# Convolutions as keys, values, queries, and the delta rule's prologue written among their products

## The chip, the cores and the metric

The kernel runs on one core of a Trainium2 chip. TensorE (PE) multiplies matrices, VectorE (DVE) and ScalarE (ACT) do elementwise work, GpSimd (POOL) a little more of it, and SyncE (SP) starts the transfers from memory. The metric is the device time of one execution in microseconds (us); lower is better.

## The reference

Two stacks of two layers each run one after the other on one sequence of 512 positions and 1024 channels. The change lies in the mixer of the second stack's layers. There the input `h` is multiplied by one wide matrix and the columns are split among three mixers: a sliding-window attention, a gated linear scan (HGRN) and a gated delta rule. The delta rule is, shortened:

```python
cqkv = jax.nn.silu(causal_depthwise_conv(cqkv, conv_w))          # width 4, 768 channels
cq, ck, cv = jnp.split(cqkv, [256, 512], axis=-1)                # 4 heads of 64 each
cq = l2norm(cq) * 64 ** -0.5
ck = l2norm(ck)
beta = jax.nn.sigmoid(cb)
g = -jnp.exp(a_log) * jax.nn.softplus(ca + dt_bias)
o_c = gated_delta_chunked(cq, ck, cv, beta, g)
# per chunk: v_new = u - w @ state ; o = q_dec @ state + qk @ v_new
#            state = g_last * state + k_dec.T @ v_new
# u, w: solutions of one triangular system whose matrix is made of the keys, beta and g
out_c = rmsnorm_2(o_c, gdn_norm) * jax.nn.silu(cg)
mixed = jnp.concatenate([out_a, out_b, out_c], axis=-1)
return mixed @ w_out
```

The matrix of the triangular system needs the keys and the gates only. The values enter as a right-hand side, the queries in `qk` and in the output.

## The kernel before

All activations are kept transposed, as tiles of 128 channels by 512 positions. Weights come as tiles of 128 by 1024 numbers: a transfer into one of three raw buffers (`wraw`), a cast by ScalarE to the upper half (`whi`, line 381) and a subtraction by VectorE for the lower half (`wlo`, line 382), each half in one of four buffers. A product (`mm3`, lines 406 to 408) is three matmuls for each of 8 tiles of input, 24 for one tile of 128 output channels. `lin_f` does such products tile by tile and hands each result, in one of four banks of PSUM with the tag `mm`, to a function `ev`.

The program is one straight list of instructions. A planner at build time puts them into the queues of the engines: the place in the list is the priority, and an instruction that the planner thinks ready may go ahead of an earlier one that it thinks is not, if a buffer of its tag is free. On the chip each queue then runs as it was written. `weave` takes turns between Python generators at each `yield`, so it sets the order in the list.

`second_mixer` computes, in this order: the inputs of the HGRN scan and the scan itself (`hgrn`), with the products for the windowed attention and the gates listed around it; the attention's rotation and factors up to its yield of "ready" (`swa`); `last[0]()`, which transposes and splits the scan's result into `y_b`; the six products `w[4:10]` for queries (outputs 4, 5), keys (6, 7) and values (8, 9), each followed by its convolution (`conv`: a copy by ScalarE, one scaling and three multiply-adds by VectorE, a tanh, one more multiply-add); then `gdn`, woven with the rest of `swa`. The output projection follows.

`gdn` begins with the gates (lines 1351 to 1373). Sums of squares of queries and keys go to one bank (line 1379), GpSimd raises them to the power -0.5 (`power`, line 1384), and `spread2` (a copy at line 682, four transposes at 676) turns a factor into a full tile with which the key tiles are multiplied (line 1390). The key tiles are copied into zero-padded tiles `kz`. For the right-hand sides `rhs` values and keys are transposed (`to_f`, line 713) and multiplied by columns (1412, 1415, 1417). Then four blocks of 128 positions are worked, woven step by step. The first steps of `block` are: decay matrix from transposed gates (1438, 1441) and a transfer of identities into one `whi` and one `wlo` buffer; key products (1450) and their scaling (1452); a transpose (1457) and two masked copies (1458, 1459); query-key products (1463, 1464) and their transpose (1468). Then six rounds of two matmul steps and a transpose (1476, 1481, 1487, with copies at 1477, 1482, 1488), the solution with the right-hand sides (1492), and `wt` (1501). The state then runs over the blocks, and the output is made.

Of the kernel before, what the change touches and what calls it, by code (L numbers as in the profile page):

```python
# [13 lines left out]
ALU = mybir.AluOpType  # L14
# [3 lines left out]
P = 128  # L18
SEQ = 512
NB = SEQ // P  # L20
# [3 lines left out]
EPS = 1e-6  # L24
# [225 lines left out]
class Net:  # L250
# [1092 lines left out]
        last.append(lambda: [self.split(early.to_f([hs[:, b].rearrange("p a b -> p (a b)") for b in range(NB)])) for hs in done])  # L1343


    def gdn(self, x, cg, ba, l, out):
        nc, V, G = self.nc, self.nc.vector, self.nc.gpsimd
        T = nc.tensor
        early = self.using(pst="mm")

        sh = (P, NB, 4)
        beta, u, g = (self.small(sh, n, 2) for n in ("gb", "gu", "gg"))
# [10 lines left out]
        ps = self.ps("mm")  # L1363
# [3 lines left out]
        gc, eg, el, gl = (self.small(sh, n, 2) for n in ("gc", "geg", "gel", "ggl"))  # L1367
        f = lambda y: y.rearrange("p a b -> p (a b)")
# [2 lines left out]
        V.tensor_tensor(f(el), ps[:, 16:32], f(gc), op=ALU.subtract)  # L1371
        nc.scalar.activation(out=eg, in_=gc, func=AF.Exp)
        nc.scalar.activation(out=el, in_=el, func=AF.Exp)

        st = self.ps("mm")
        for i in range(4):
            sq = self.square(x[i], "ns")
            for b in range(NB):
                T.matmul(st[:, 8 * b + 2 * i:8 * b + 2 * i + 2], sq[:, b * P:(b + 1) * P], self.bd64[:, 0:65:64], start=True, stop=True)
        rs_ = self.small((P, 32), "gms", 2)  # L1380
        V.tensor_scalar(rs_, st[:, 0:32], EPS, None, op0=ALU.add)
        rs3, rn = rs_.rearrange("p (a b) -> p a b", a=NB), self.small((P, NB, 8), "grn", 2)
        def power(c):
            G.tensor_tensor(rn[:, :, c], rs3[:, :, c], self.nhalf[:, 0:32].rearrange("p (a b) -> p a b", a=NB)[:, :, c], op=ALU.pow)

        power(slice(4, 6))
        power(slice(6, 8))
        for i in range(2, 4):
            ps = early.spread2(rn[:, :, 2 * i:2 * i + 2])
            V.tensor_tensor(x[i], x[i], ps, op=ALU.mult)  # L1390
            yield
        power(slice(0, 4))
        rq = self.small((P, NB, 4), "grq", 2)
        V.tensor_scalar(rq, rn[:, :, 0:4], 0.125, None, op0=ALU.mult)
        q, k, vf = x[0:2], x[2:4], x[4:6]
        kz2 = [self.big((P, 2, SEQ), "gk") for _ in range(2)]
        kz = [kz2[h // 2][:, h % 2, :] for h in range(4)]
        for h, t in enumerate(kz):
            r, n = slice(64 * (h % 2), 64 * (h % 2) + 64), slice(64 - 64 * (h % 2), 128 - 64 * (h % 2))
            G.memset(t[n, :], 0.0)  # L1400
            nc.scalar.copy(t[r, :], k[h // 2][r, :])

        eb = self.small(sh, "geb", 2)
        V.tensor_tensor(eb, beta, eg, op=ALU.mult)
        rhs, kd = [], []
        for i in range(2):
            hh = slice(2 * i, 2 * i + 2)
            bc = lambda y: y[:, :, hh].unsqueeze(3).to_broadcast([P, NB, 2, 64])
            r = self.big((P, NB, 2, 128), name="grhs")
            ps = early.to_f([vf[i][:, b * P:(b + 1) * P] for b in range(NB)])  # L1410
            v4 = ps.rearrange("p (a b c) -> p a b c", a=NB, b=2)
            V.tensor_tensor(r[:, :, :, 0:64], v4, bc(beta), op=ALU.mult)
            ps = early.to_f([k[i][:, b * P:(b + 1) * P] for b in range(NB)])
            k4 = ps.rearrange("p (a b c) -> p a b c", a=NB, b=2)
            V.tensor_tensor(r[:, :, :, 64:128], k4, bc(eb), op=ALU.mult)
            t = self.t((P, NB, 2, 64), name="gkd")
            V.tensor_tensor(t, k4, bc(el), op=ALU.mult)
            rhs.append(r)
            kd.append(t)
            yield  # L1420
        m0, m1, m2 = self.mats("lv64", 4), self.mats("lv4", 4), self.mats("later", 2)
# [6 lines left out]
        p4 = lambda y: y.rearrange("p (a b) -> p a b", a=4)  # L1428
        QT, uw = [None] * NB, [None] * NB
        wt = [self.t(name="gwt") for _ in range(2)]  # L1430

        yield

        def block(b):
            s = slice(b * P, (b + 1) * P)
# [67 lines left out]
                    nc.scalar.copy(wt[i][:, s], ps[:, i * P:(i + 1) * P])  # L1503
            yield

        yield from weave(*(block(b) for b in range(NB)))

        sbd = {}
        for i in range(2):
            state = None  # L1510
            for c in range(NB - 1):
                ps = self.ps("mx")
                for p in range(2):
                    r = slice(64 * p, 64 * p + 64)
# [6 lines left out]
                else:  # L1521
                    m = self.t((P, P), name="gmt", tag="x")
                    G.memset(m, 0.0)
                    for p in range(2):
                        r = slice(64 * p, 64 * p + 64)
                        V.scalar_tensor_tensor(m[r, r], self.ident[r, r], gl[r, c, 2 * i + p:2 * i + p + 1], ps[r, 64 + 64 * p:128 + 64 * p],
                                               op0=ALU.mult, op1=ALU.subtract)
# [10 lines left out]
                for p in range(2):  # L1538
                    r = slice(64 * p, 64 * p + 64)
# [3 lines left out]
        for b in range(NB):  # L1543
# [16 lines left out]
            else:  # L1560
                t = self.t((P, 4, 64), name="got", tag="x")
                V.tensor_tensor(t, o3(po[:, 256:512]), eg[:, b, :].unsqueeze(2).to_broadcast([P, 4, 64]), op=ALU.mult)
                V.tensor_tensor(hs[:, 0], t, o3(p2[:, 0:256]), op=ALU.add)
            r = self.head_rstd(hs, (1, 4), rq[:, b:b + 1, :])
# [142 lines left out]
    def second_mixer(self, x, l):  # L1707
        nc, V, G = self.nc, self.nc.vector, self.nc.gpsimd
        keep = {}

        def ev(o, ps):
            if 4 <= o < 10:
                keep[o] = L.conv(ps, self.vec("conv_w2", l)[:, 4 * (o - 4):4 * (o - 4) + 4], 3, None)
                return
            t = keep[o] = L.t(name="u")
            if o < 4:
                nc.scalar.copy(t, ps)
                return
# [12 lines left out]

        def gate(t, ps):

            nc.scalar.activation(out=t, in_=ps, func=AF.Tanh, scale=0.5)
            V.scalar_tensor_tensor(t, t, 1.0, ps, op0=ALU.add, op1=ALU.mult)

        def evt0(b, ps):
            nc.scalar.copy(bv[:, b, :], ps[:, 0:256])
            gate(bg[:, b, :], ps[:, 256:512])

        def evt1(b, ps):
            nc.scalar.copy(av[:, b, :], ps[:, 0:128])
            gate(cg[:, b, :], ps[:, 128:384])
            V.tensor_copy(ba[:, b, :], ps[:, 384:392])

        w = self.tiled("win2_f", l, KD)
        y_a, y_c, last = [], [], []

        def gains(t, n):
            t4 = t.rearrange("p a (b c) -> p (a b) c", b=4)  # L1750
            G.tensor_tensor(t4, t4, self.row(n, l).unsqueeze(1).to_broadcast([P, 16, 64]), op=ALU.mult)

        self.lin_f(w[0:4], x, ev, wide=4)
        gh = self.using("m", "mx").hgrn([keep[2], keep[3]], [keep[0], keep[1]], bv, bg, l, last)
        for n, _ in enumerate(self.lin_t_steps(self.d["win2_t0"][l], x, 512, evt0)):
            if n + 1 in (7, 8):
                next(gh)
        for n, _ in enumerate(gh):
            if n == 2:
                gains(bg, "hgrn_norm")  # L1760
        self.lin_t(self.d["win2_t1"][l], x, 392, evt1)
        gains(cg, "gdn_norm")
        self.lin_f(w[10:15], x, lambda o, ps: ev(o + 10, ps))
        ga = self.using("l", "mx").swa([keep[o] for o in range(10, 14)], keep[14], keep["st"], av, l, self.tab2, y_a)
        while next(ga) != "ready":
            pass
        y_b = last[0]()
        self.lin_f(w[4:10], x, lambda o, ps: ev(o + 4, ps))
        gc = self.using("m", "mm").gdn([keep[o] for o in range(4, 10)], cg, ba, l, y_c)
        drain(weave(gc, ga))  # L1770
        return y_a + y_b + y_c

# [48 lines left out]
def weave(*gens):  # L1821

    gens = list(gens)
    while gens:
        for g in list(gens):
            try:
                new = next(g)
            except StopIteration:
                gens.remove(g)
            else:  # L1830
                if new is not None:
                    gens.append(new)
                yield


def drain(gen):
    for _ in gen:
        pass
# [25 lines left out]
```

## Time and profile before

| | us |
|---|---|
| median of three executions | 3587.05 |
| lowest and highest | 3585.47, 3589.41 |
| the profiled execution: its time | 3586.55 |
| the profiled execution: its span | 3584.7 |
| TensorE busy | 3484.3 |
| VectorE busy | 1989.1 |
| ScalarE busy | 1364.5 |
| GpSimd busy | 140.5 |

The span is the time from the first to the last instruction of one execution that the hardware profiler recorded. The mean clock granted to TensorE in it is 0.992 of full speed. The second mixer runs twice, once in each layer of the second stack; the key products of `gdn` (line 1450) begin at 2317.6 us in the first pass, and the last of them in the second begins at 3060.7 us. In the rows below a line of the profile names the engine, the line of the kernel, the output and the inputs by the program's names, and `<-` followed by an engine and a line says what ended a wait.

### The profile page before, as it was taken

The numbers are of one execution on the slowest core, as the hardware profiler recorded it, in microseconds if no ns is written. First come the engines' busy times: TensorE is split into PE (matmuls) and PEld (weight loads), VectorE is DVE, ScalarE is ACT, GpSimd is POOL, SyncE is SP. The second block draws the span as 40 slices with busy tenths as digits, with TensorE's granted clock in tenths as the row PEclk, the third lists the DMA queues.
The fourth block names the chain that finished last, engine by engine and source line by source line (L and its number), as shares of the span: only waits on it lengthen the run. The fifth ranks groups of instructions, "written<-read, shape, count | busy, mean of one in ns | idle before, by whom it ended". The sixth has DMA issues, their size and how long they took to land.

```text
span 3584.7 us, 44503 instructions
## 1 busy us (share of the span) xinstructions
PE 3484.3 (97%) x17694; PEld 2901.8 (81%) x17694; DVE 1989.1 (55%) x3074; ACT 1364.5 (38%) x2231; POOL 140.5 (4%) x130
## 2 busy tenths in 40 slices
PE   9999999999999999999999998899999989999999
PEld 7888777888888888777888887788888877888887
DVE  6555665554665555674556577756333475654333
ACT  4223454323333223463223364354222453543221
POOL 0000000000000000000000003100000021000000
PEclk9999999999999999999999999899999999999999
DMA  5444212444334443202444321102333222022332
GB/s 167 141 135 129 84 32 68 142 145 128 127 100 142 146 138 100 91 15 95 146 148 137 94 77 54 62 7 75 108 98 101 78 71 68 1 71 90 100 99 83
DMA packets 114272, 349.06 MB, mean 97 GB/s; under 512 B 11536, under 2 KB 27920, under 8 KB 114064
## 3 DMA queue, kind: packets, MB, share of 16 engines
q1 hardware_dynamic: 114064, 346.21, 30.8%
q8 instruction: 140, 2.29, 0.3%
q14 instruction: 68, 0.56, 0.0%
HBM read 339.87 MB, written 2.10 MB: 95 GB/s over the span
## 4 chain that ended last, share of the span: by engine, by line
PE 87%; DVE 6%; issue 3%; ACT 2%; POOL 1%; DMA 1%; SPq 0%; POOLq 0%; DVEq 0%; ACTq 0%
PE mm L406 24%; PE mm L408 24%; PE mm L407 24%; PE mm L1481 1%; PE mm L1476 1%; PE mm L476 1%; PE mm L477 1%; PE mm L475 1%; PE mx L968 1%; DVE hacc L1279 1%; DVE wlo L382 1%; PE mm L809 1%; PE mx L948 1%; ACT sc L1138 1%; PE mx L1121 1%
## 5 line engine op out<-in xcount | busy, mean ns | idle before, releaser
L381 ACT CAST whi<-wraw 128x1024 fp32r<-128x1024 f32 (+3 forms) x540 | 553.4, 1029 | 1553.6 <-PE mm L407 1271.7
L406 PE MATMUL mm<-xh,whi 128*128 128x512 f32 (+1 forms) x2784 | 1053.3, 380 | 9.7 <-ACT whi L381 6.4
L407 PE MATMUL mm<-xl,whi 128*128 128x512 f32 (+1 forms) x2784 | 1055.8, 380 | 1.6 <-DVE xl L588 1.4
L408 PE MATMUL mm<-xh,wlo 128*128 128x512 f32 (+1 forms) x2784 | 1055.8, 380 | 0.3 <-DVE wlo L382 0.3
L382 DVE TENSOR_TENSOR wlo<-wraw,whi 128x1024 fp32r<-128x1024 f32 (+3 forms) x540 | 643.7, 1194 | 274.9 <-ACT whi L381 234.3
L406 PEld LDWEIGHTS mm<-xh,whi 128*128 128x128 f32 x2784 | 522.4, 189 | 107.8 <-ACT whi L381 6.4
L407 PEld LDWEIGHTS mm<-xl,whi 128*128 128x128 f32 x2784 | 524.9, 189 | 100.3 <-DVE xl L588 2.5
L408 PEld LDWEIGHTS mm<-xh,wlo 128*128 128x128 f32 x2784 | 524.8, 189 | 100.4 <-DVE wlo L382 3.1
L408 PE MATMUL mm<-hi,wlo 128*128 128x512 f32 (+1 forms) x1390 | 532.2, 383 | 2.1 <-DVE wlo L382 2.1
L406 PE MATMUL mm<-hi,whi 128*128 128x512 f32 (+1 forms) x1390 | 532.5, 384 | 0.2
L407 PE MATMUL mm<-lo,whi 128*128 128x512 f32 (+1 forms) x1390 | 531.8, 383 | 0.0
L408 PEld LDWEIGHTS mm<-hi,wlo 128*128 128x128 f32 x1390 | 261.3, 188 | 54.2 <-DVE wlo L382 4.2
L406 PEld LDWEIGHTS mm<-hi,whi 128*128 128x128 f32 x1390 | 261.1, 188 | 51.4 <-ACT hi L399 1.1
L407 PEld LDWEIGHTS mm<-lo,whi 128*128 128x128 f32 x1390 | 261.3, 188 | 50.3
L658 DVE SCALAR_TENSOR_TENSOR h<-mm,h 128x512 f32<-128x512 f32 x112 | 77.2, 691 | 224.2 <-PE mm L408 224.1
L1589 DVE SCALAR_TENSOR_TENSOR ada<-wraw,cond,ada 128x1024 f32<-128x1024 f32 x84 | 107.9, 1284 | 95.6 <-DMA wraw<-in_ada_w_dram 95.2
L637 DVE TENSOR_TENSOR gl<-mm,rstd 128x512 f32<-128x512 f32 x88 | 60.7, 690 | 155.1 <-PE mm L408 155.1
L636 DVE TENSOR_TENSOR silu<-mm,rstd 128x512 f32<-128x512 f32 x88 | 60.7, 689 | 145.2 <-PE mm L408 145.2
L658 DVE SCALAR_TENSOR_TENSOR h<-mm,mod,h 128x512 f32<-128x512 f32 (+1 forms) x70 | 48.9, 704 | 148.7 <-PE mm L408 148.7
L399 ACT CAST hi<-gl 128x512 fp32r<-128x512 f32 x132 | 82.2, 623 | 100.6 <-DVE gl L639 99.9
L633 DVE TENSOR_TENSOR gl<-silu,mm 128x512 f32<-128x512 f32 x44 | 30.2, 687 | 135.8 <-PE mm L408 135.8
L400 DVE TENSOR_TENSOR lo<-gl,hi 128x512 fp32r<-128x512 f32 x132 | 90.5, 686 | 15.4 <-ACT hi L399 15.4
(493 smaller groups left out, 3606.2 us busy)
## 6 DMA issues: line engine op xcount, KB each, us to landing
wraw<-in_ffn_gate_dram SPq DMA_DIRECT2D x130, 512.0 KB, 3.5
wraw<-in_ffn_up_dram SPq DMA_DIRECT2D x130, 512.0 KB, 4.0
wraw<-in_ada_w_dram SPq DMA_DIRECT2D x96, 512.0 KB, 3.7
wraw<-in_ffn_down_dram SPq DMA_DIRECT2D x96, 448.0 KB, 3.3
wraw<-in_win_f_dram SPq DMA_DIRECT2D x50, 512.0 KB, 3.5
wraw<-in_ffn_down_dram SPq DMA_DIRECT2D x48, 512.0 KB, 3.5
wraw<-in_w_out_dram SPq DMA_DIRECT2D x32, 512.0 KB, 3.5
wraw<-in_win_t_dram SPq DMA_DIRECT2D x16, 512.0 KB, 3.5
```

Of the source, the lines that this page charges most:

```text
L381: self.nc.scalar.copy(hi[:, s], raw)
L382: self.nc.vector.tensor_tensor(lo[:, s], raw, hi[:, s].bitcast(F32), op=ALU.subtract)
L399: self.nc.scalar.copy(hi, src)
L400: self.nc.vector.tensor_tensor(lo, src, hi.bitcast(F32), op=ALU.subtract)
L406: T.matmul(ps, whi, xhi, start=first, stop=False)
L407: T.matmul(ps, whi, xlo, start=False, stop=False)
L408: T.matmul(ps, wlo, xhi, start=False, stop=last)
L475: T.matmul(ps, xh[:, bs], w[0][:, s], start=k == 0, stop=False)
L636: nc.vector.tensor_tensor(sg, gate_ps, rb, op=ALU.mult)
L637: nc.vector.tensor_tensor(gg, up_ps, rb, op=ALU.mult)
L658: self.nc.vector.scalar_tensor_tensor(h, ps[:, c], scale, h, op0=ALU.mult, op1=ALU.add)
L1589: V.scalar_tensor_tensor(acc, raw, cond[:, k:k + 1], acc, op0=ALU.mult, op1=ALU.add)
```

## The change

The products and convolutions come in the order keys, values, queries, and `gdn` gets the dictionary `keep` in place of the six finished tiles, so that it can be started before they are all there. `gdn` now yields "values" and "queries" where it needs them. Between the keys' and the values' products stand its gates, the factors of the keys, the padded keys, the key part of the right-hand sides, the masks, and the first two steps of blocks 0 and 1. Between the values' and the queries' products stand the values' part of the right-hand sides and the third step of these two blocks. The factors of the queries and all else follow the queries' products. `factors` replaces the joint sum of squares for four tiles; it is called once for the two key tiles and once for the two query tiles. `y_b` is made after the last product. Lines that only move are cut.

```diff
-    def gdn(self, x, cg, ba, l, out):
+    def gdn(self, keep, cg, ba, l, out):
...
-        st = self.ps("mm")
-        for i in range(4):
-            sq = self.square(x[i], "ns")
-            for b in range(NB):
-                T.matmul(st[:, 8 * b + 2 * i:8 * b + 2 * i + 2], sq[:, b * P:(b + 1) * P], self.bd64[:, 0:65:64], start=True, stop=True)
...
-        power(slice(4, 6))
-        power(slice(6, 8))
-        for i in range(2, 4):
-            ps = early.spread2(rn[:, :, 2 * i:2 * i + 2])
-            V.tensor_tensor(x[i], x[i], ps, op=ALU.mult)
-            yield
-        power(slice(0, 4))
...
+        def factors(tiles):
+
+            st = self.ps("mm")
+            for i, x in enumerate(tiles):
+                sq = self.square(x, "ns")
+                for b in range(NB):
+                    T.matmul(st[:, 4 * b + 2 * i:4 * b + 2 * i + 2], sq[:, b * P:(b + 1) * P], self.bd64[:, 0:65:64], start=True, stop=True)
+            ss, r = self.small(sh, "gms", 2), self.small(sh, "grn", 2)
+            V.tensor_scalar(f(ss), st[:, 0:16], EPS, None, op0=ALU.add)
+            for c in (slice(0, 2), slice(2, 4)):
+                G.tensor_tensor(r[:, :, c], ss[:, :, c], self.nhalf[:, 0:16].rearrange("p (a b) -> p a b", a=NB)[:, :, c], op=ALU.pow)
+            return r
...
+        k = [keep[6], keep[7]]
+        rk = factors(k)
...
+        for i in range(2):
+            ps = early.spread2(rk[:, :, 2 * i:2 * i + 2])
+            V.tensor_tensor(k[i], k[i], ps, op=ALU.mult)
+            yield
...
+        rhs, kd = [self.big((P, NB, 2, 128), name="grhs") for _ in range(2)], []
         for i in range(2):
-            ps = early.to_f([vf[i][:, b * P:(b + 1) * P] for b in range(NB)])
-            v4 = ps.rearrange("p (a b c) -> p a b c", a=NB, b=2)
-            V.tensor_tensor(r[:, :, :, 0:64], v4, bc(beta), op=ALU.mult)
             ps = early.to_f([k[i][:, b * P:(b + 1) * P] for b in range(NB)])
             k4 = ps.rearrange("p (a b c) -> p a b c", a=NB, b=2)
+            V.tensor_tensor(rhs[i][:, :, :, 64:128], k4, bc(eb, i), op=ALU.mult)
...
-        yield from weave(*(block(b) for b in range(NB)))
+        blocks = [block(b) for b in range(NB)]
+
+        for n in range(2):
+            for b in range(2):
+                next(blocks[b])
+        yield "values"
+        for i in range(2):
+            ps = early.to_f([keep[8 + i][:, b * P:(b + 1) * P] for b in range(NB)])
+            V.tensor_tensor(rhs[i][:, :, :, 0:64], ps.rearrange("p (a b c) -> p a b c", a=NB, b=2), bc(beta, i), op=ALU.mult)
+        for b in range(2):
+            next(blocks[b])
+        yield "queries"
+        q.extend([keep[4], keep[5]])
+        r_, rq = factors(q), self.small((P, NB, 4), "grq", 2)
+        V.tensor_scalar(rq, r_, 0.125, None, op0=ALU.mult)
+        yield from weave(*blocks)
...
+        gc = self.using("m", "mm").gdn(keep, cg, ba, l, y_c)
+
+        self.lin_f(w[6:8], x, lambda o, ps: ev(o + 6, ps))
+        while next(gc) != "values":
+            pass
+        self.lin_f(w[8:10], x, lambda o, ps: ev(o + 8, ps))
+        while next(gc) != "queries":
+            pass
+        self.lin_f(w[4:6], x, lambda o, ps: ev(o + 4, ps))
         y_b = last[0]()
-        self.lin_f(w[4:10], x, lambda o, ps: ev(o + 4, ps))
-        gc = self.using("m", "mm").gdn([keep[o] for o in range(4, 10)], cg, ba, l, y_c)
         drain(weave(gc, ga))
```

## Rows read from the trace of the kernel before

**Rows 1.** The page: busy time of each engine, share of the span, instructions.

```profile
PE 3484.3 (97%) x17694; PEld 2901.8 (81%) x17694; DVE 1989.1 (55%) x3074; ACT 1364.5 (38%) x2231; POOL 140.5 (4%) x130
```

**Rows 2.** Stretches: bounds, length, busy PE, PEld, DVE, ACT, POOL; clock; DMA.

```profile
2250.60:2287.20 36.60, 35.28 (x166) 28.92 (x165) 30.66 (x55) 13.87 (x21) 7.64 (x2) 1.00 0.28 86
2287.20:2346.60 59.40, 46.68 (x309) 39.84 (x308) 49.81 (x120) 25.80 (x66) 6.86 (x4) 0.83 0.07 21
2346.60:2372.10 25.50, 23.90 (x210) 20.80 (x208) 13.92 (x34) 20.22 (x56) 1.23 (x5) 1.00 0.00 1
3025.50:3086.00 60.50, 47.77 (x308) 40.80 (x308) 49.70 (x120) 25.89 (x66) 6.86 (x4) 0.80 0.07 20
```

**Rows 3.** TensorE's waits in stretch B of the first pass: total us, times, longest.

```profile
PE mx L1121 <- DVE sc L1124: 3.0, 1, 3.0
PE mm L676 <- ACT sp L682: 3.0, 2, 2.5
PE mm L1463 <- DVE gm L1459: 2.9, 2, 2.3
PE mm L1450 <- ACT sc L1138: 2.0, 1, 2.0
PE mm L713 <- DVE cout L844: 1.5, 1, 1.5
```

**Rows 4.** TensorE in order of time: start, us, instruction, idle before and its releaser.

```profile
2287.55 2.82 PE L1379 MATMUL mm<-base,sq 128*128 128x2 f32 x24
...
2317.57 5.51 PE L1450 MATMUL mm<-gk 128*128 128x128 f32 x32 [1.95 <-ACT sc L1138]
```

**Rows 5.** Slices of ten microseconds, columns as in group 2.

```profile
2290.00:2300.00 10.00, 7.46 (x36) 6.25 (x35) 4.44 (x10) 2.47 (x5) 3.70 (x3) 0.75 0.24 77
2300.00:2310.00 10.00, 4.92 (x19) 3.66 (x19) 8.73 (x17) 4.62 (x8) 2.84 (x1) 0.50 0.00 1
2310.00:2320.00 10.00, 8.05 (x48) 7.41 (x48) 10.00 (x31) 4.37 (x15) 0.00 (x0) 0.84 0.00 1
```

**Rows 6.** VectorE's groups in stretch B: busy us, mean ns, idle before and releaser.

```profile
L1124 DVE TENSOR_TENSOR sc<-mx,mats 128x512 f32<-128x512 f32 (+1 forms) x12 | 7.3, 618 | 0.0
...
L1126 DVE TENSOR_REDUCE wm<-sc 128x2 f32<-128x512 f32 (+1 forms) x12 | 7.3, 610 | 0.0
...
L1143 DVE TENSOR_TENSOR sc<-sc,wr 128x512 f32<-128x512 f32 (+1 forms) x8 | 4.4, 622 | 0.0
...
L1390 DVE TENSOR_TENSOR cout<-cout,mm 128x512 f32<-128x512 f32 x2 | 1.4, 686 | 3.4 <-PE mm L676 3.4
...
L1452 DVE SCALAR_TENSOR_TENSOR gm<-mm,gnb,ge 128x128 f32<-128x128 f32 x16 | 4.7, 342 | 0.0
...
L1459 DVE COPY_PREDICATED gm<-mats,mm 128x512 f32<-128x512 int32 x4 | 2.9, 725 | 0.0
```

**Rows 7.** VectorE in order of time, first pass.

```profile
2255.67 0.67 DVE L1087 TENSOR_TENSOR u<-u,ro 128x512 f32<-128x512 f32 x1
...
2277.87 0.69 DVE L844 SCALAR_TENSOR_TENSOR cout<-cout,cacc 128x512 f32<-128x512 f32 x1 [0.70 <-ACT cout L843]
```

**Rows 8.** TensorE in order of time, inside the iteration.

```profile
2372.12 3.84 PE L1481 MATMUL mm<-gm,gm 128*128 128x128 f32 x32
```

**Rows 9.** GpSimd in order of time, first pass.

```profile
2253.99 7.64 POOL L1080 TENSOR_TENSOR srn<-sms,nhalf 128x8 f32<-128x8 f32 x2 [21.48 <-DVE sms L1077]
...
2296.30 6.54 POOL L1384 TENSOR_TENSOR grn<-gms,nhalf 128x8 f32<-128x8 f32 x3 [34.67 <-DVE gms L1381]
```

**Rows 10.** TensorE's waits in stretch A of the first pass.

```profile
PE mx L676 <- ACT sp L682: 1.3, 1, 1.3
```

**Rows 11.** Three slices of 20 us of the gated scan, 2160 to 2220, summed.

```profile
sum 60.00, PE 50.04 PEld 40.74 DVE 56.53 ACT 24.71 POOL 24.28; mean PE 16.68 PEld 13.58 DVE 18.84 ACT 8.24 POOL 8.09
```

**Rows 12.** ScalarE in order of time: one cast of a weight tile.

```profile
2250.45 1.05 ACT L381 CAST whi<-wraw 128x1024 fp32r<-128x1024 f32 x1 [4.45 <-PE mm L407]
```

**Rows 13.** VectorE's groups in stretch A: the other half of the casts.

```profile
L382 DVE TENSOR_TENSOR wlo<-wraw,whi 128x1024 fp32r<-128x1024 f32 x3 | 3.7, 1221 | 5.3 <-PE mm L713 5.3
```

More of the change, by code (lines that the diff above doesn't have):

```diff
@@ L1373, in gdn @@
         nc.scalar.activation(out=el, in_=el, func=AF.Exp)
-        st = self.ps("mm")
-        for i in range(4):
-            sq = self.square(x[i], "ns")
-            for b in range(NB):
-                T.matmul(st[:, 8 * b + 2 * i:8 * b + 2 * i + 2], sq[:, b * P:(b + 1) * P], self.bd64[:, 0:65:64], start=True, stop=True)
[L1380 to L1384, printed above, removed]
-        power(slice(4, 6))
-        power(slice(6, 8))
-        for i in range(2, 4):
-            ps = early.spread2(rn[:, :, 2 * i:2 * i + 2])
-            V.tensor_tensor(x[i], x[i], ps, op=ALU.mult)
-            yield
-        power(slice(0, 4))
-        rq = self.small((P, NB, 4), "grq", 2)
-        V.tensor_scalar(rq, rn[:, :, 0:4], 0.125, None, op0=ALU.mult)
-        q, k, vf = x[0:2], x[2:4], x[4:6]
+        def factors(tiles):
[11 more added lines that the diff above has]
+        rk = factors(k)
         kz2 = [self.big((P, 2, SEQ), "gk") for _ in range(2)]
@@ L1398, in gdn @@
         for h, t in enumerate(kz):
-            r, n = slice(64 * (h % 2), 64 * (h % 2) + 64), slice(64 - 64 * (h % 2), 128 - 64 * (h % 2))
-            G.memset(t[n, :], 0.0)
+            G.memset(t[64 - 64 * (h % 2):128 - 64 * (h % 2), :], 0.0)
+        for i in range(2):
+            ps = early.spread2(rk[:, :, 2 * i:2 * i + 2])
+            V.tensor_tensor(k[i], k[i], ps, op=ALU.mult)
+            yield
+        for h, t in enumerate(kz):
+            r = slice(64 * (h % 2), 64 * (h % 2) + 64)
             nc.scalar.copy(t[r, :], k[h // 2][r, :])
@@ L1404, in gdn @@
         V.tensor_tensor(eb, beta, eg, op=ALU.mult)
-        rhs, kd = [], []
+        bc = lambda y, i: y[:, :, 2 * i:2 * i + 2].unsqueeze(3).to_broadcast([P, NB, 2, 64])
+        rhs, kd = [self.big((P, NB, 2, 128), name="grhs") for _ in range(2)], []
         for i in range(2):
-            hh = slice(2 * i, 2 * i + 2)
-            bc = lambda y: y[:, :, hh].unsqueeze(3).to_broadcast([P, NB, 2, 64])
-            r = self.big((P, NB, 2, 128), name="grhs")
-            ps = early.to_f([vf[i][:, b * P:(b + 1) * P] for b in range(NB)])
-            v4 = ps.rearrange("p (a b c) -> p a b c", a=NB, b=2)
-            V.tensor_tensor(r[:, :, :, 0:64], v4, bc(beta), op=ALU.mult)
             ps = early.to_f([k[i][:, b * P:(b + 1) * P] for b in range(NB)])
             k4 = ps.rearrange("p (a b c) -> p a b c", a=NB, b=2)
-            V.tensor_tensor(r[:, :, :, 64:128], k4, bc(eb), op=ALU.mult)
+            V.tensor_tensor(rhs[i][:, :, :, 64:128], k4, bc(eb, i), op=ALU.mult)
             t = self.t((P, NB, 2, 64), name="gkd")
-            V.tensor_tensor(t, k4, bc(el), op=ALU.mult)
-            rhs.append(r)
+            V.tensor_tensor(t, k4, bc(el, i), op=ALU.mult)
             kd.append(t)
@@ L1430, in gdn @@
         wt = [self.t(name="gwt") for _ in range(2)]
-        yield
+        q = []
         def block(b):
```

## The prediction, made before the changed kernel was seen

> **What bounds the kernel now.** I read the page first. TensorE is busy for 97% of the span [rows 1], so on the average the kernel is bound by its products, and another order of the other work can only win where TensorE stands still or runs at a low clock. The change touches the second mixer alone, which runs twice, so I cut each pass into stretches and asked for their busy times [rows 2]. A (36.6 us) holds the six products for keys, values and queries; B (59.4 us, 60.5 in the second pass) is the prologue of the delta rule up to the first matmul of its iteration; C (25.5 us) is the iteration while the windowed attention still runs beside it. The reader is to see that A idles for 1.3 us and C for 1.6, and that B idles for 12.7 us in each pass, at a mean granted clock of 0.83 and 0.80.
>
> What B waits for is in the list of waits [rows 3]: 3.0 us for the copies ahead of the spread of the key factors (L676), 1.5 us for a convolution that VectorE has not finished (L713), 3.0 us for scores behind the same convolutions (L1121), 2.0 us before the key products (L1450), 2.9 us for the masked copies (L1463). In order of time it is one chain, from the sums of squares at 2287.55 to the key products at 2317.57 [rows 4], and it starts only when the last of the six products is through. The clock follows the pause: 0.75, 0.50 and 0.84 in the slices of ten microseconds from 2290 on [rows 5]; 0.50 is the lower of the two levels, 1.2 GHz, for a whole slice. What that costs is busy time multiplied by the missing share: 7.46 x 0.25 + 4.92 x 0.50 + 8.05 x 0.16 = 5.6 us. Idle and clock together are 12.7 + 5.6 = 18.3 us a pass. The B of the second pass repeats the first within a microsecond or so [rows 2]; I work one pass and double it.
>
> VectorE is the other engine to watch: 30.7 us of A and 49.8 us of B [rows 2]. Of the latter the windowed attention's own masks, maxima and scalings are 7.3 + 7.3 + 4.4 = 19.0 us [rows 6], which nobody needs before C.
>
> **The change, part by part.** *Order of the convolutions.* The same six products and six convolutions are issued; nothing is added. The first two convolutions of today end on VectorE at 2278.5 [rows 7], the other four behind them. In the new order those first two are the keys, so squares, power and spread can begin at about 2278 and not, as now, at 2287.55, behind the last product [rows 4]. From 2278 on one to two products are still to run, each at most 5.9 us (35.28 busy over six, [rows 2]).
>
> *The factors.* Two calls for two tiles each in place of one for four. VectorE gains one small add, below 0.2 us. GpSimd still takes 32 columns to the power -0.5, which last 6.54 us in three calls today [rows 9], so a call for 8 columns, of which there will be four, is about 1.6 us. GpSimd has no other work in B, and the first two calls stay ahead of the spread as they are.
>
> *The key part of the right-hand sides, the masks, two blocks up to their first masked copies.* All of it moves ahead of the values' or the queries' product. On TensorE that is 8 transposes for the spread, 8 of keys, 8 of the cumulated gates, 8 key products and 8 transposes of a block, each 0.12 us at full clock (32 in 3.84, [rows 8]): 4.8 us that leave B and enter A. On VectorE it is two scalings and four multiplications of 0.69, twice eight small ones of 0.34 and four masked copies of 0.73 [rows 6]: 4.1 + 5.4 + 2.9 = 12.4 us that enter A, where it has 36.6 - 30.7 = 5.9 us free [rows 2]. So the query convolutions slide into B, as the value ones do now. What matters is that B then begins with two blocks whose matrices are ready; each has 24 + 24 + 20 matmuls of iteration, 68 x 0.12 = 8.2 us, to fill gaps with.
>
> *What leaves.* If the chain lies beside the products, four of the five waits go, 3.0 + 1.5 + 3.0 + 2.0 = 9.5 us, and without a pause of that length the clock's 5.6 us: 15.1 us a pass. The 2.9 us at L1463 stay, since the last two blocks begin where they did.
>
> *What comes back.* TensorE takes its queue in order. An instruction of the key chain that stands among the products and is not ready holds the products behind it. One such place exists in A today, the spread of the attention's key factors, and costs 1.3 us [rows 10]. The new places are the sums of squares, two spreads, the key products and the blocks' transposes: 5 x 1.3 = 6.5 us. The other reading is a stretch in which products are already threaded through a chain of GpSimd, ScalarE and VectorE, the gated scan at the head of this mixer: 50.04 us busy of 60 [rows 11], 17% lost while products wait behind; 17% of A and the 4.8 us is 7.0 us. The bounds are nothing (each is placed late enough) and more than the 15.1 us; the two readings agree, and I take 7.0.
>
> *Weights.* The two early blocks hold two of the four pairs of weight buffers while values and queries are multiplied. Today a cast is done several tiles ahead: the one at 2250.45 waited only for a product that released its buffer, and it lasts 1.05 us [rows 12], and VectorE's half 1.22 us [rows 13]. With two pairs a buffer comes free when the tile two before has been used, so both halves have one product, 5.5 us or so, to be done in. Priced at nothing: cover 5.5 - 2.3 = 3.2 us a tile; without the cover it is a rival below. Two casts move into A with it, 2.4 us of VectorE. The identities for the early blocks wait for buffers in SyncE's queue, ahead of raw weights; those have three buffers of their own, filled before, so nothing is priced.
>
> *Late y_b.* Eight transposes and two splits move behind the queries' product. Their reader is the output projection, behind the whole iteration: nothing, and 1.4 us of VectorE leave A.
>
> *Sum.* 15.1 - 7.0 = 8.1 us a pass, 16.2 in both. The profiled execution took 3586.55 us around a span of 3584.7 us, 0.5 us below the median: 3586.55 - 16.2 = 3570.
>
> *A rule against it.* Four powers of GpSimd will run beside the busiest time of VectorE. Today two of them fill 7.64 us from 2253.99 on [rows 9], and a sum of two operands in SBUF at 2255.67 took 0.67 us and began without a gap [rows 7]. The Trainium skill, page "SBUF — State Buffer", section "Who interferes with whom", says that a VectorE instruction with two SBUF inputs contends with a GpSimd instruction that reads SBUF, and that whichever comes second is blocked until the other has ended. The trace does not agree for this operation; by the rule the gain would shrink as in the third rival.
>
> **The rivals.** *VectorE stays the bound and the idle only moves* (0.15). For it: 80.5 us busy of the 96 us of A and B, and the blocks need its masked copies. Against it: 19 us of that can wait for C, and VectorE itself idles for 3.4 us inside the chain, for the spread [rows 6]. Stalls of 12 to 18 us a pass in place of 7 leave a gain of 3 to a loss of 3: 3580 to 3593. It would end in the same place if the queue stayed much as it is, because a product that is ready goes ahead of a chain that is not.
>
> *Weights starve* (0.14), the case that ends slower. Where VectorE's half of a cast stands over 3.2 us deep behind convolutions and the key part, it holds the next product. VectorE's surplus in A is 12.4 + 2.4 - 1.4 - 5.9 = 7.5 us, so it can happen, at up to four tiles. Against it: no product of A waits for a cast today [rows 10]. It decides when the four tiles lose more than 8.1 us together, 2.0 each; at twice that a pass is 8.1 us longer than before: 3603.
>
> *Blocked by the powers* (0.05). If each call stops VectorE while it is behind, 4 x 1.6 = 6.5 us a pass come back: 8.1 - 6.5 = 1.6, twice: 3583. The row of VectorE above speaks against it. It is what the page of the Trainium skill named above would make of this kernel.
>
> *Everything overlaps* (0.06). No new stalls, and L1463 and C's 1.6 us go too: 18.3 + 1.6 = 19.9 a pass, 3547.
>
> **How the numbers follow.** The forecast has 0.60, with its own range from 3556 (nothing comes back, 2 x 15.1) to 3581 (12.5 us come back a pass). A measurement of this kernel can tell about 0.2%, 7 us, from no change. Faster by more: the forecast, the full overlap and a little of the rest, 0.67. Within: most of the first and third rivals, 0.18. Slower: the weights and a little of the first, 0.15. The range 3550 to 3594 leaves out most of the full overlap and most of the starving.
>
> **What the changed profile would show.** Right: key products start before the last query product ends, the waits of L676 and L713 shrink or stand among products, the clock stays near 1.00, and the iteration's first matmul comes well before 59 us after the last product. "What leaves" is wrong if the clock still falls to 0.50 behind the products. "What comes back" is wrong if the key chain's instructions wait more than 8 us among the products. Starving would show as products that wait for L381 or L382. The forecast as a whole is wrong if A grows by as much as B shrinks.

## The result and the profile after

The changed kernel takes 3619.82 us (median of four, 3614.48 to 3622.64), the kernel before 3586.99 beside it: a ratio of 1.0088 [1.0076, 1.0101]. It is slower by 33 us, 50 us above the forecast and 26 above the upper end of the range. The profiled execution, the fastest of the four, has a span of 3612.7 us, 28.0 more than that of before; the lines below account for these 28.0.

The page's busy times, to be held against [rows 1]:

```profile
PE 3491.2 (97%) x17694; PEld 2907.3 (80%) x17694; DVE 1989.3 (55%) x3076; ACT 1366.1 (38%) x2231; POOL 140.3 (4%) x132
```

The work is the same: no engine gains more than 7 us; TensorE's 6.9 go with a mean clock of 0.989 in place of 0.992. So TensorE stands still longer. To find where, I cut the mixer from the attention's last sum of squares to the output's last transpose, both outside the moved work. Stretches of the kernel before, columns as in group 2:

```profile
2253.40:2446.60 193.20, 175.36 (x1253) 153.59 (x1253) 125.94 (x281) 88.45 (x208) 19.97 (x16) 0.95 0.11 34
2991.40:3185.70 194.30, 176.45 (x1253) 154.61 (x1252) 125.90 (x280) 88.53 (x208) 19.99 (x16) 0.94 0.11 34
```

The same stretches of the changed kernel, then the slices of ten microseconds in which its clock falls:

```profile
2256.00:2461.70 205.70, 176.76 (x1254) 153.84 (x1253) 128.83 (x281) 91.45 (x211) 19.91 (x17) 0.93 0.10 31
3006.90:3212.60 205.70, 176.71 (x1254) 153.85 (x1253) 128.79 (x281) 91.58 (x211) 19.92 (x17) 0.93 0.10 32
...
2270.00:2280.00 10.00, 3.73 (x16) 3.56 (x16) 5.01 (x10) 3.48 (x9) 0.96 (x1) 0.60 0.00 0
2280.00:2290.00 10.00, 8.13 (x40) 7.34 (x41) 6.38 (x16) 4.76 (x8) 2.28 (x2) 0.54 0.01 2
...
2300.00:2310.00 10.00, 3.79 (x18) 2.67 (x16) 8.41 (x13) 2.68 (x4) 0.00 (x0) 0.81 0.24 70
2310.00:2320.00 10.00, 9.80 (x44) 8.58 (x45) 3.12 (x6) 1.16 (x3) 0.00 (x0) 0.85 0.13 47
```

A pass is 12.5 and 11.4 us longer, 23.9 of the 28.0. TensorE's idle time in the first goes from 193.20 - 175.36 = 17.8 to 205.70 - 176.76 = 28.9 us. Another 2.6 us lie ahead of the first pass, where the change does nothing (last section), 1.5 between and behind the passes.

TensorE in order of time after the keys' product (L1380 is the keys' sums of squares, L676 their spread, L1442 the key products, L713 at 2310.20 the values' transposes):

```profile
2267.92 0.37 PE L1366 MATMUL mm<-gg,base 128*128 128x16 f32 x2
2272.74 1.87 PE L1380 MATMUL mm<-base,sq 128*128 128x2 f32 x8 [4.44 <-ACT sq L663]
2276.88 1.87 PE L1380 MATMUL mm<-base,sq 128*128 128x2 f32 x8 [2.27 <-ACT sq L663]
2281.38 1.11 PE L676 MATMUL mm<-base,sp 128*128 128x128 f32 x4 [2.63 <-ACT sp L682]
...
2287.56 2.71 PE L1442 MATMUL mm<-gk 128*128 128x128 f32 x16
2290.02 0.47 PE L406 MATMUL mm<-xh,whi 128*128 128x512 f32 x1
...
2292.83 0.50 PE L408 MATMUL mm<-xh,wlo 128*128 128x512 f32 x1 [1.64 <-DVE wlo L382]
...
2310.20 1.11 PE L713 MATMUL mm<-base,cout 128*128 128x128 f32 x4 [5.03 <-DVE cout L844]
```

No matmul of a product stands between 2268 and 2290. The list has the key chain (gates, sums of squares, power, spread, key products) ahead of the values' product, and the queue has it so too: the whole chain is worked with nothing to fill its waits, though the values' product needs none of its results. The values' transposes stand ahead of the queries' product in the same way, and there TensorE waits 5.03 us for a convolution. The list of TensorE's waits of this pass (line, releaser: total us, times, longest); of the 7.1 us at L1380, 6.7 stand in the key chain and 0.35 before the queries' sums, behind the products:

```profile
PE mm L1380 <- ACT sq L663: 7.1, 3, 4.4
PE mm L713 <- DVE cout L844: 6.4, 2, 5.0
PE mx L1158 <- DVE sc L1143: 3.8, 2, 3.6
PE mm L676 <- ACT sp L682: 3.1, 2, 2.6
...
PE mm L408 <- DVE wlo L382: 1.6, 1, 1.6
```

VectorE in order of time tells the other side of the chain:

```profile
2256.29 0.20 DVE L1077 TENSOR_SCALAR sms<-mx 128x40 f32<-128x40 f32 x1 [11.59 <-PE mx L1731]
...
2278.78 0.17 DVE L1382 TENSOR_SCALAR gms<-mm 128x16 f32<-128x16 f32 x1 [2.62 <-PE mm L1380]
2282.53 0.69 DVE L1396 TENSOR_TENSOR cout<-cout,mm 128x512 f32<-128x512 f32 x1 [3.58 <-PE mm L676]
...
2291.56 2.35 DVE L382 TENSOR_TENSOR wlo<-wraw,whi 128x1024 fp32r<-128x1024 f32 x2
```

It idles for 11.59 us before most of the attention's rotations, then inside the chain (2.62 and 3.58 us), and the values' lower halves come only behind all of it, at 2291.56: the 1.64 us at L408.

### The profile page after: what moved, and what is told of

Same layout as the page of the kernel before. It is cut to its first block, busy times and chain, and to the rows that moved or that the text cites. A ratio compares the mean times of both kernels' runs of the same rounds, so it can differ in the third digit from the quotient of the medians.

```text
span 3612.7 us, 44509 instructions
## 1 busy us (share of the span) xinstructions
PE 3491.2 (97%) x17694; PEld 2907.3 (80%) x17694; DVE 1989.3 (55%) x3076; ACT 1366.1 (38%) x2231; POOL 140.3 (4%) x132
## 4 chain that ended last, share of the span: by engine, by line
PE 84%; DVE 8%; issue 3%; ACT 2%; POOL 1%; DMA 1%; SPq 0%; POOLq 0%; DVEq 0%; ACTq 0%
PE mm L406 24%; PE mm L408 24%; PE mm L407 24%; PE mm L1473 1%; PE mm L1468 1%; DVE wlo L382 1%; PE mx L968 1%; DVE hacc L1279 1%; DVE cacc L841 1%; PE mm L476 1%; PE mm L477 1%; PE mm L475 1%; PE mm L809 1%; PE mx L948 1%; PE mx L1330 1%
## 5 line engine op out<-in xcount | busy, mean ns | idle before, releaser
L408 PE MATMUL mm<-xh,wlo 128*128 128x512 f32 (+1 forms) x2784 | 1056.3, 380 | 3.6 <-DVE wlo L382 3.5
L408 PEld LDWEIGHTS mm<-xh,wlo 128*128 128x128 f32 x2784 | 525.4, 189 | 104.5 <-DVE wlo L382 7.2
L408 PE MATMUL mm<-hi,wlo 128*128 128x512 f32 (+1 forms) x1390 | 531.6, 383 | 2.1 <-DVE wlo L382 2.1
L408 PEld LDWEIGHTS mm<-hi,wlo 128*128 128x128 f32 x1390 | 261.3, 188 | 53.6 <-DVE wlo L382 3.6
L400 DVE TENSOR_TENSOR lo<-gl,hi 128x512 fp32r<-128x512 f32 x132 | 90.4, 685 | 15.1 <-ACT hi L399 15.1
```

The lines of the kernel that those rows point to most:

```text
L400: self.nc.vector.tensor_tensor(lo, src, hi.bitcast(F32), op=ALU.subtract)
L408: T.matmul(ps, wlo, xhi, start=False, stop=last)
```

## The experiments

Three theories went in. Q: TensorE's queue keeps the order of the list, and the chain stands in it in front of products that are ready. W: the early blocks hold weight buffers, and casts come late. V: VectorE bounds the prologue, and any order moves the idle time about. Each kernel was timed beside the kernel before, whose median moved between 3586.99 and 3590.58 us, so kernels of different experiments are best compared by their ratios to it.

**No early blocks.** Each block begins behind the queries' product; the rest of the change stays.

```diff
-        for n in range(2):
-            for b in range(2):
-                next(blocks[b])
         yield "values"
...
-        for b in range(2):
-            next(blocks[b])
         yield "queries"
```

> The changed kernel without the two early blocks: all four blocks begin behind the queries' product, so no weight buffer is held by a block while values and queries are multiplied. Theory Q (queue order: the key chain is listed ahead of the values' product, TensorE takes its queue in order and stands still for the key convolutions, the power and the spread): sums of squares still wait about 7 us a pass and the spreads about 3 us; 3600 to 3620. Theory W (weights: the blocks hold two of the four pairs, so the values' weights are cast too late and the product can only come behind the chain): the waits of the key chain go, and the kernel is at or below the one before, 3570 to 3588.

Measured: 3626.70 us, 1.0097 [1.0082, 1.0112]. The first waits of its list:

```profile
PE mm L1380 <- ACT sq L663: 10.7, 4, 7.4
PE mm L713 <- DVE cout L844: 5.1, 1, 5.1
PE mm L676 <- ACT sp L682: 3.1, 2, 2.6
```

The time is above the range of either theory. But the buffers are free and the time is no better, so W falls as the cause: the second of the values' two lower halves is cast at 2252.49, before the keys' product ends, and the values' first matmul still comes at 2286.40, behind the chain.

```profile
2252.49 1.23 DVE L382 TENSOR_TENSOR wlo<-wraw,whi 128x1024 fp32r<-128x1024 f32 x1 [5.35 <-ACT whi L381]
```

The waits of the chain are all there, as Q has it. The early blocks cost nothing in sum here; if anything they help.

**Weights listed first.** The values' weight tiles are loaded and cast in the list ahead of the key chain.

```diff
-                w = self.load(src, nt * kt * P)
+                w = src if isinstance(src, tuple) else self.load(src, nt * kt * P)
...
         self.lin_f(w[6:8], x, lambda o, ps: ev(o + 6, ps))
+        w[8:10] = [(self.load(src, KD * P), 1) for src, _ in w[8:10]]
         while next(gc) != "values":
```

> The changed kernel with the loads and casts of the two value weight tiles listed ahead of the delta rule's key part, the early blocks kept. Theory Q: the product still stands behind the key chain in TensorE's queue, only the 1.6 us for the lower half of a cast go; 3612 to 3622. Theory W: with the weights ready in time the product no longer has to come late; 3570 to 3595.

Measured: 3616.71 us, 1.0067 [1.0050, 1.0084]. The wait at L408 is gone, and those of L1380 (8.4), L713 (6.4) and L676 (3.1) stay. The loss goes from 0.88% to 0.67% with overlapping intervals, so a gain isn't shown, and most of the loss is left. The trace shows again that the weights did not hold the product. The second of the values' two lower halves is cast at 2251.18, and the product's first matmul comes 35 us later, behind the key products (L1442):

```profile
2251.18 1.23 DVE L382 TENSOR_TENSOR wlo<-wraw,whi 128x1024 fp32r<-128x1024 f32 x1 [5.35 <-ACT whi L381]
```

```profile
2285.27 2.19 PE L1442 MATMUL mm<-gk 128*128 128x128 f32 x16
2287.21 0.48 PE L406 MATMUL mm<-xh,whi 128*128 128x512 f32 x1
```

**Values' product ahead of the chain.** Both insertions now stand between the values' and the queries' products.

```diff
         self.lin_f(w[6:8], x, lambda o, ps: ev(o + 6, ps))
-        while next(gc) != "values":
-            pass
         self.lin_f(w[8:10], x, lambda o, ps: ev(o + 8, ps))
         while next(gc) != "queries":
```

> The changed kernel with the values' product listed ahead of the key part, so 11 us of products stand between the keys' product and their sums of squares; everything else, the early blocks too, as in the change. Theory Q: the 7.1 us before the sums of squares shrink below 3, the spreads' 3 us and the 6.4 us at the transposes stay, since only the power and the value convolutions are waited for there; 3590 to 3606. Theory W: the pairs are held as before and the casts of values and queries are as late; 3612 to 3625.

Measured: 3593.58 us (ten runs), 1.0008 [0.9998, 1.0017]. One product moved, with every other instruction kept, takes the loss from 0.88% to 0.08%, which the interval doesn't tell from nothing. Three waits of its list:

```profile
PE mm L676 <- ACT sp L682: 3.6, 2, 3.1
...
PE mm L1380 <- ACT sq L663: 2.0, 2, 1.7
...
PE mm L713 <- DVE gm L1451: 1.1, 2, 0.6
```

The sums of squares lose their wait (7.1 to 2.0) because the convolutions now end beside a product; the chain's own latency through GpSimd and ScalarE (L676) does not go, since nothing is listed beside it. I expected the 6.4 us at the values' transposes (L713) to stay, and they fell to 1.1: the key chain, listed ahead of these transposes now, covers the values' convolutions. The time and the squares' wait are as Q has them.

**Order only.** Order keys, values, queries, all of the delta rule behind all products, no early blocks (the diff above for the early blocks, and):

```diff
         self.lin_f(w[6:8], x, lambda o, ps: ev(o + 6, ps))
-        while next(gc) != "values":
-            pass
         self.lin_f(w[8:10], x, lambda o, ps: ev(o + 8, ps))
-        while next(gc) != "queries":
-            pass
         self.lin_f(w[4:6], x, lambda o, ps: ev(o + 4, ps))
+        while next(gc) != "queries":
+            pass
```

> The order keys, values, queries alone: all of the delta rule behind the queries' product, no early blocks. Theory Q: nothing of the chain stands among the products, the key convolutions are done when the chain begins, so it starts no later than in the kernel before; 3570 to 3590. A theory that the new order itself costs (the query convolutions, now last, hold the query-key products, or VectorE is the bound whatever the order): 3592 to 3615.

Measured: 3586.14 us (ten runs), 0.9990 [0.9980, 0.9999]. The order of the products alone costs nothing. Nor does the rest of the change, the two calls of `factors` and the late `y_b`, which this kernel keeps.

**Attention's rotations behind the key convolutions.** They are listed after the keys' product instead of before it.

```diff
-        while next(ga) != "ready":
-            pass
         gc = self.using("m", "mm").gdn(keep, cg, ba, l, y_c)
         self.lin_f(w[6:8], x, lambda o, ps: ev(o + 6, ps))
+        while next(ga) != "ready":
+            pass
         while next(gc) != "values":
```

> The changed kernel with the attention's rotations listed behind the key convolutions, so VectorE, idle until then, does the keys first. Theory Q (TensorE stands at the key chain because VectorE has the keys late): the waits before the sums of squares fall from 7.1 us a pass to below 3; the power's 3 us and the values' transposes stay; 3603 to 3614. If the sums of squares wait as long as before, something else than VectorE's order holds them: 3616 to 3624.

Measured: 3617.34 us, 1.0082 [1.0066, 1.0097], a miss: the time lies in the other theory's range, though the squares' wait does not stay. The wait at L1380 shrinks to 4.2 us, but the spread of the attention's key factor, now behind the product too, waits 2.4 in place of 1.3, and L408 2.3 in place of 1.6. L713 (6.4) is as it was. Moving one piece of the chain mostly moved the wait.

**The chain threaded through the products.** Early blocks kept; `factors` is cut in two, and the pieces stand between single products.

```diff
-        rk = factors(k)
+        st = squares(k)
+        yield "squares"
+        rk = powers(st)
...
         for n in range(2):
+            if n:
+                yield "chain"
             for b in range(2):
                 next(blocks[b])
...
         self.lin_f(w[6:8], x, lambda o, ps: ev(o + 6, ps))
-        while next(gc) != "values":
+        self.lin_f(w[8:10], x, lambda o, ps: ev(o + 8, ps))
+        while next(gc) != "squares":
             pass
-        self.lin_f(w[8:10], x, lambda o, ps: ev(o + 8, ps))
+        self.lin_f(w[4:5], x, lambda o, ps: ev(o + 4, ps))
+        while next(gc) != "chain":
+            pass
+        self.lin_f(w[5:6], x, lambda o, ps: ev(o + 5, ps))
         while next(gc) != "queries":
             pass
-        self.lin_f(w[4:6], x, lambda o, ps: ev(o + 4, ps))
```

> Everything of the change kept, but the key chain cut into pieces between single products: keys, values, sums of squares, first query tile, spread to gates, second query tile, key products and the values' part. Theory Q: with a product of 5.5 us in front of each piece the waits for squares and spread go, below 3 us a pass together, and with the early blocks it ends below the kernel before: 3570 to 3586. If the idle only moves to VectorE's side: 3588 to 3600.

Measured: 3583.55 us (ten runs), 0.9987 [0.9977, 0.9996]. Its first waits, and three stretches of 20 us:

```profile
PE mx L1158 <- DVE sc L1143: 3.8, 2, 3.6
PE mm L713 <- DVE cout L1400: 2.2, 2, 1.7
PE mx L1121 <- DVE kz L1106: 1.9, 1, 1.9
PE mm L1453 <- DVE gm L1448: 1.7, 2, 1.1
```

```profile
2290.00:2310.00 20.00, 15.84 (x80) 12.90 (x80) 17.44 (x38) 8.68 (x16) 0.00 (x0) 0.83 0.27 81
2310.00:2330.00 20.00, 16.37 (x112) 14.42 (x111) 17.19 (x42) 5.43 (x9) 3.25 (x2) 0.91 0.00 1
2330.00:2350.00 20.00, 16.20 (x121) 13.32 (x120) 17.12 (x43) 14.20 (x44) 0.00 (x0) 0.91 0.01 2
```

The waits ahead of the keys' sums of squares are gone and L676 is at 0.9 us, and 36 us of the changed kernel's time with them. Most of what is left is released by VectorE, which is busy for 17 of every 20 us: this points to V for the remainder, and the last experiment tests it.

**Order and early blocks.** The early blocks stay and all of the delta rule is listed behind the last product (the diff of "order only" without its first part).

> The order keys, values, queries with the delta rule behind all products, and the two early blocks as in the change. Theory Q: as the order alone (a few us below the kernel before) plus what the early blocks give, which between the change and its version without them was 3 to 9 us in the two passes: 3576 to 3586. If the early blocks cost, by holding weights or by their order: 3588 to 3600.

Measured: 3582.21 us (ten runs), 0.9979 [0.9969, 0.9989], 7.5 us below before, the best so far (the interval overlaps that of the threaded kernel), with the chain not among the products at all. The early blocks go with a wait of their own: in the first pass of all six kernels so far that have them TensorE waits 3.3 to 3.8 us at L1158, the transposes of the attention's scores, and 0.4 in the two with the new order and without them. GpSimd and VectorE of this run, for the powers:

```profile
2293.06 3.30 POOL L1384 TENSOR_TENSOR grn<-gms,nhalf 128x8 f32<-128x8 f32 x2 [27.23 <-DVE gms L1382]
```

```profile
2293.77 0.69 DVE L844 SCALAR_TENSOR_TENSOR cout<-cout,cacc 128x512 f32<-128x512 f32 x1
...
2294.89 0.75 DVE L841 SCALAR_TENSOR_TENSOR cacc<-conv,vecs,cacc 128x509 f32<-128x509 f32 x1
```

Two operations with two inputs run inside the 3.30 us of power, at the 0.69 and 0.75 us that they take elsewhere, the first in the middle of a power; the two powers for the queries take 3.24 us in the same run.

**Values' part late.** Of the changed kernel only the second insertion is undone: the values' right-hand sides and the third step of the early blocks come behind the queries' product.

```diff
         self.lin_f(w[8:10], x, lambda o, ps: ev(o + 8, ps))
-        while next(gc) != "queries":
-            pass
         self.lin_f(w[4:6], x, lambda o, ps: ev(o + 4, ps))
+        while next(gc) != "queries":
+            pass
```

> The changed kernel with only the second insertion undone: the values' part and the blocks' transposes behind the queries' product, the key chain where the change has it. Theory Q: the 6.4 us a pass at the values' transposes go, the 10 us at squares and spreads stay; 3604 to 3612. If these waits only move: 3616 to 3622.

Measured: 3601.88 us, 1.0038 [1.0023, 1.0053], just below the range that I gave Q. The wait at L713 is gone, those of the key chain stay (L1380 6.8, L676 3.1). So the insertions share the loss: 18 us hang on the second, and the first accounts for what is left.

**Rotations as they come.** V says that VectorE's time is worth something in the prologue. Each attention tile is rotated right behind its own product, among the attention's products, where VectorE has idle time (the 11.59 us above), in four kernels: the threaded one, order and early blocks, the one before, the changed one. The same four lines go from `swa`.

```diff
                 nc.tensor.matmul(keep["st"][:, 10 * b + 2 * i:10 * b + 2 * i + 2], ...)
+            r = L.t(name="ro", tag="sq")
+            V.stream_shuffle(r, t, TURN_8)
+            V.tensor_tensor(r, r, self.tab2[1], op=ALU.mult)
+            V.tensor_tensor(t, t, self.tab2[0], op=ALU.mult)
+            V.tensor_tensor(t, t, r, op=ALU.add)
```

> The threaded version (key chain in pieces between single products) with the attention's rotations listed tile by tile behind the attention's own products, into time in which VectorE stands idle; 10 to 12 us of VectorE work a pass leave the stretch of the convolutions. Theory V (with the queue's waits gone VectorE is the bound of the prologue, so the overlap gained little): the prologue shortens by 4 to 8 us a pass against the threaded version; 3566 to 3577. If VectorE is not the bound there: as the threaded version, 3580 to 3588.

> The order keys, values, queries with two early blocks and the delta rule behind all products, and the same earlier rotations. Theory V: 4 to 8 us a pass below the same version without them; 3566 to 3576. If the chain's own latency behind the products is the bound and VectorE is not: 3578 to 3586.

> The kernel before with the earlier rotations alone. Theory V: VectorE reaches the end of the six convolutions sooner, 3 to 6 us a pass; 3575 to 3584. If the product of queries, keys and values is what is waited for: 3586 to 3591, unchanged.

> The changed kernel with the earlier rotations. Theory Q (the key chain stands in front of the values' product and waits for the key convolutions, which VectorE has late because of the rotations): the wait before the sums of squares falls from 7.1 us a pass to below 4, the power's 3 us and the values' transposes' 6 us stay; 3604 to 3614. If the rotations are not what makes the keys late: 3616 to 3622.

Measured, beside 3589.07 for the kernel before:

| rotations early in | us | ratio | without them |
|---|---|---|---|
| threaded | 3573.32 | 0.9956 [0.9942, 0.9969] | 0.9987 |
| order and early blocks | 3577.55 | 0.9967 [0.9955, 0.9980] | 0.9979 |
| before | 3579.83 | 0.9976 [0.9966, 0.9985] | 1 |
| changed | 3613.03 | 1.0070 [1.0058, 1.0083] | 1.0088 |

The first beats both kernels, by 16 and 46 us. Its two passes:

```profile
2254.70:2441.30 186.60, 173.42 (x1251) 150.73 (x1250) 117.14 (x261) 89.74 (x209) 20.97 (x17) 0.96 0.12 35
2987.50:3171.60 184.10, 171.46 (x1251) 149.34 (x1251) 117.00 (x261) 89.83 (x209) 20.99 (x17) 0.98 0.12 36
```

They are 6.6 and 10.2 us shorter than those of before. Three of the four times lie in the range of the theory that I held; order and early blocks, at 3577.55, lies in neither of its two, and its intervals with and without the rotations overlap. The two gains add up: 0.13% for threading and 0.24% for the rotations in the kernel before make 0.37%, inside the interval of the 0.44% measured. The threaded kernel does not need the rotations more than the old one does, so this pair does not show that VectorE alone held it. In the changed kernel the sums of squares (L1375 there) still wait 5.5 us where I expected less than 4. With the rotations gone, VectorE's queue still has other work of the attention ahead of the key convolutions, and waits there for GpSimd's powers:

```profile
2266.39 0.18 DVE L1088 TENSOR_SCALAR srn<-srn 128x32 f32<-128x32 f32 x1 [6.93 <-POOL srn L1080]
```

The first key convolution starts behind it, at 2267.08, and TensorE's queue has no product beside the convolutions.

## Why the prediction was wrong, by its own steps

**"What leaves" held, and was worth nothing by itself.** The waits of stretch B [rows 3] did leave the place behind the last product, and the iteration's first matmul comes at 2340.0, 16 us behind the last product and not 59. I had named that as a sign of being right. It was a poor one: measured from the attention's last sum, the last matmul of that iteration line comes after 171.0 us (2256.0 to 2427.0), before after 154.3. Nor is the old place free of new waits: the 3.8 us at L1158, which the list of the kernel before doesn't have, stand there.

**"What comes back" is the step that failed.** I put it at 7.0 us a pass (6.5 by the other reading), between nothing and more than the 15.1 that leave. Among the products TensorE now waits 6.7 (L1380) + 3.1 (L676) + 6.4 (L713) + 1.6 (L408) = 17.8 us, over twice the 8 us that I had named as the sign of being wrong. By the sum: of the 17.8 us idle before, 9.5 were to leave, so 28.9 - 8.3 = 20.6 came back, the 3.8 us at L1158 among them, and with them the clock, 3.73 x 0.40 + 8.13 x 0.46 + 3.79 x 0.19 + 9.80 x 0.15 = 7.4 us against 5.6 that left. That is 28.0 against 15.1, 12.9 a pass where the pass grew by 12.5 and 11.4.

Both rows that I sized it by were the wrong neighbours. The 1.3 us of [rows 10] and the 17% of [rows 11] are stalls of chains whose steps have products *between* them. Here no product lies between the steps: the list puts all of the chain ahead of the values' product, and my sum starts from "If the chain lies beside the products" without a reason why it would. My own sentence, that an instruction which is not ready holds the products behind it, was right; I priced it by stalls of one step each, and here the steps add up. Nearer was the price of the same chain alone in the queue, the 18.3 us of stretch B itself [rows 2], in the kernel I was reading. Moving the values' product ahead (1.0008) and undoing the second insertion (1.0038) show this on the chip; leaving out early blocks (1.0097) and listing the weights first (1.0067), with the product behind the chain in both although its weights were cast, rule out the buffers as the main cause.

**"Order of the convolutions" had the start right and the cover wrong.** I let the key chain begin at about 2278 [rows 7], with one to two products still to run. The second key convolution ends at 2276, so the start is about as forecast, but the keys' product ends at 2268 and no other product runs: for most of these 8 us TensorE waits for convolutions that products had hidden.

**"Weights", priced at nothing,** cost the 1.6 us at L408 a pass. The rival in which they starve gave 3603, slower as it came out, but for another reason than the one that made the kernel slower; no rival reached 3620. Early blocks, its supposed cause, gain 4 us when nothing else is moved (3586.14 to 3582.21, with intervals that overlap).

**"VectorE stays the bound"** fits the remainder, but isn't shown. With the queue's waits taken out by threading, a gain of 0.13% is left where I forecast 0.45%, and most of the waits left are for VectorE; yet earlier rotations gave this kernel about as much (0.31%) as the old one (0.24%). "Idle only moves" is too kind to the change as made: with 28.9 us of it in place of 17.8 in the first pass, it grew.

**"Blocked by the powers"** did not happen. In the changed kernel VectorE has nothing to do while the keys' powers run (the 3.58 us above); the rows of order and early blocks show two-input operations at their usual times beside a power. The Trainium skill, page "SBUF — State Buffer", section "Who interferes with whom", would have the second of such a pair wait for the first; these rows do not agree.

Open: why the planner kept the products behind a chain that was not ready. It did so even with the values' weights listed and cast first. The queue's order is plain in the trace, the planner's estimates behind it are not, and no run here tested them, nor whether it lacked a free `mm` bank.

## What to carry to other kernels

Listing a dependent chain ahead of independent products did not overlap the two here: TensorE's queue worked the chain alone where no products stood between its steps. So write the order as it should run, one product between a step and the one that waits for it. Price such a move by what the chain costs with nothing beside it, which the old profile showed here at the old place, and only then subtract what is listed between its steps. And look for cover on the other engines first: rotating tiles where VectorE idled gained 9 us in the kernel before without touching the chain.

## What was not expected of the hardware

The same pause cost the clock in one execution and not in the other. Ahead of L1273, in the gated scan, TensorE waits 2.55 us in the kernel before and 2.54 in the changed one. The first matmuls behind it and the five microseconds that follow, before and then after:

```profile
2162.88 1.16 PE L1273 MATMUL mx<-hq,hk 64*128 64x128 f32 x16 [2.55 <-DVE hk L1265]
...
2165.00:2170.00 5.00, 5.00 (x39) 4.62 (x38) 4.78 (x6) 1.67 (x3) 1.06 (x1) 1.00 0.30 104
```

```profile
2163.40 2.08 PE L1273 MATMUL mx<-hq,hk 64*128 64x128 f32 x16 [2.54 <-DVE hk L1265]
...
2165.00:2170.00 5.00, 5.00 (x21) 4.78 (x18) 2.98 (x5) 1.57 (x3) 1.21 (x2) 0.53 0.32 108
```

Both are busy throughout, one with 39 matmuls at a clock of 1.00, the other with 21 at 0.53, near the lower level of 1.2 GHz. By these rows that costs 5.00 x 0.47 = 2.35 us (an estimate), the larger part of the 2.6 us which the changed kernel had lost before its first moved instruction. TensorE was busy throughout the five microseconds ahead of 2160 in both, at a clock of 1.00; with one execution of each, why the clock fell in one alone stays open.
